# A hybrid trunk's attention: fp32r tiles and fp32r transposes for the softmax weights of the first half

## The chip, the cores and the metric

The kernel runs on one core of one Trainium2 chip. The metric is device time in microseconds (us), the median of repeated runs. The profile and its trace show one execution, with the engines PE (matmuls; PEld its weight loads), DVE (VectorE), ACT (ScalarE), POOL (GpSimd) and SP (SyncE).

## What is computed

A trunk of two layers over 1024 latent tokens and 256 context tokens, of width 1024: a convolution layer and an attention layer, each followed by a dense SwiGLU layer, all in fp32. The change lies in the attention, of which the core is this:

```python
def gqa_sdpa(q, k, v):                      # 16 query heads, 4 kv heads, head width 64
    qg = q.reshape(B, Q, N_KV_HEADS, KV_GROUP, Dh)
    s = jnp.einsum("bqkgd,bskd->bkgqs", qg, k).astype(jnp.float32) * (Dh ** -0.5)
    p = jax.nn.softmax(s, axis=-1).astype(v.dtype)
    o = jnp.einsum("bkgqs,bskd->bqkgd", p, v)
    return o.reshape(B, Q, H * Dh)
```

Each query reads all 1280 keys (1024 latent and 256 context), and the output passes through a projection `wo`.

## The kernel before

**Products in pairs.** The kernel keeps the operands of its matmuls as a high part, the fp32 value cast to the type fp32r, and a low part, the difference to the fp32 value, and sums the products of the parts. ACT casts, DVE subtracts.

**Units.** The 1024 queries run in two halves of 512. A half has 16 units: a kv head t and a block of 128 queries, and in a unit the four query heads that share t. `attn_stream` makes the list of steps. In a unit `scores` (L1105) does, for each head, six matmul rows against 1280 keys (L1116) into PSUM, DVE's scaling into the head's softmax slot in SBUF with the row's minimum beside it (L1122), and ACT's exponent in place, with the row sum (L1124). `values` (L1128) then takes the four slots through ten key blocks: PE transposes the block of each head, 128x128, into one PSUM bank (L1134, four transposes in f32 against an identity), ACT copies the bank as the high part (L1137), DVE subtracts for the low part (L1138), and PE adds both to the output (L1140, L1141). Two banks take the transposes in turn, four buffer pairs the parts. At the end of the unit come the reciprocal of the sums (DVE, L1145), its spread on POOL (L1147), two copies and two adds (ACT L1151, DVE L1152), two transposes and the product (L1155, L1156), and the store to `od` (POOL, L1450). The `values` of a unit run beside the `scores` of the next: three, three, three and two steps of it behind each of its heads (`turns`). The value products carry a later priority (`later`, 40 steps). A scheduler fixes from this one order for each engine, and waits are put where data or buffers ask for them; every engine then works through its own list in order.

**The slots.** The first half's slots come from a ring of places in three big tiles, T1, HS and T5 (`pring`). Units 0 to 2 run beside the last query projection; from unit 3 on attention runs alone. A unit takes four slots that the unit before does not hold, one by one. A slot is taken over when the first transpose of the last key block to read it is done, since the scaling of the next user writes it.

**Around it.** The queries of a unit come by a DMA on POOL's queue (L1102). When the first half is done, `out_proj` loads its output from `od` into the tile HS (L1485), splits it into high and low parts in tiles tagged T6 and T3 (`split`: ACT L161, DVE L164), and multiplies by `wo` (L172 to L174), beside the second half's attention, which uses slots of T1 and T5 again.

## Time and profile before

| | |
|---|---|
| median of 3 runs | 2941.39 us (2937.71 to 2943.6) |
| profiled execution | 2938.98 us |
| its span, first to last instruction | 2937.2 us |
| mean granted TensorE clock | 0.987 |
| busy: PE, PEld, DVE, ACT, POOL | 97%, 83%, 74%, 45%, 8% |
| first half, units 4 to 14 (1671.35 to 1833.42) | 162.07 us |
| f32 transposes L1134 in the trace | 1280 |

A row of a group gives line, engine, operation, tiles and shapes, count, then busy time and mean ns of one, then the idle time before them with what ended it. A timeline row gives start, duration, engine, line, operation, and in square brackets the idle time ahead of it and its releaser; x2 is two in a row. The ends of matmuls are modelled, so for PE and DVE the distance from start to start says more than a duration.

### The profile page before, as it was taken

To read this page: it belongs to the slowest core of one execution; us is meant where nothing else is said; L and a number is where in the kernel's file an instruction comes from. 1 tells how busy PE (TensorE), PEld (TensorE's weight loads), DVE (VectorE), ACT (ScalarE), POOL (GpSimd) and SP (SyncE) were. 2 spreads that over 40 slices of the span, in tenths; PEclk is the share of its full clock that TensorE was granted. 3 is DMA by queue.
4 is the path that set the end of the run, shared out by engine and by line. 5 is a ranking of instruction groups with operands and counts; after the bars stand their busy time and mean duration, and the time that the engine had idled before them with its cause. 6 is when DMAs were issued, how large, how long until landed. Compare 5 with 4: busy or idle time off the path is not lost.

```text
span 2937.2 us, 42731 instructions
## 1 busy us (share of the span) xinstructions
PE 2847.7 (97%) x16462; PEld 2446.1 (83%) x16462; DVE 2160.7 (74%) x3746; ACT 1335.5 (45%) x2229; POOL 222.6 (8%) x377
## 2 busy tenths in 40 slices
PE   7999989999999999999999999989999999999998
PEld 6888877888888889989888787767777778889997
DVE  6887788847556378877786899786666666786777
ACT  5222255532222245544445688645555543444444
POOL 0000001011022001000011111110000000010000
PEclk9999999999999999999999999999999999999999
DMA  6443444334356224333345211322222143353332
GB/s 249 140 120 98 116 131 145 135 116 143 115 175 198 65 74 165 114 104 112 109 156 170 88 46 46 97 87 81 66 73 83 60 149 99 110 170 104 102 98 75
DMA packets 131755, 336.58 MB, mean 115 GB/s; under 512 B 31328, under 2 KB 52864, under 8 KB 130656
## 3 DMA queue, kind: packets, MB, share of 16 engines
q1 hardware_dynamic: 78016, 222.33, 24.1%
q0 software_dynamic: 29344, 103.83, 10.7%
q10 hardware_dynamic: 24192, 7.70, 1.1%
q8 instruction: 129, 2.11, 0.3%
q14 instruction: 74, 0.61, 0.1%
HBM read 289.50 MB, written 38.93 MB: 112 GB/s over the span
## 4 chain that ended last, share of the span: by engine, by line
PE 86%; DVE 7%; ACT 2%; issue 2%; DMA 2%; ACTq 0%; POOL 0%; SPq 0%; DVEq 0%; POOLq 0%
PE ps L172 15%; PE ps L173 15%; PE ps L174 15%; PE ps L875 4%; PE ps L877 4%; PE ps L876 4%; PE ps L1116 4%; PE ps L1134 4%; PE ps L1140 2%; PE ps L454 2%; PE ps L455 2%; PE ps L456 2%; PE ps L1141 2%; PE ps L185 1%; PE ps L183 1%
## 5 line engine op out<-in xcount | busy, mean ns | idle before, releaser
L172 PE MATMUL ps<-T,wh 128*128 128x512 f32 (+1 forms) x1360 | 502.5, 370 | 1.4 <-ACT T L161 0.8
L174 PE MATMUL ps<-T,wl 128*128 128x512 f32 (+1 forms) x1360 | 500.4, 368 | 2.0 <-DVE wl L148 2.0
L173 PE MATMUL ps<-T,wh 128*128 128x512 f32 (+1 forms) x1312 | 481.4, 367 | 0.2 <-DVE T L164 0.2
L144 ACT CAST wh<-wr 128x1024 fp32r<-128x1024 f32 (+1 forms) x217 | 225.0, 1037 | 419.9 <-PE ps L173 307.2
L148 DVE TENSOR_TENSOR wl<-wr,wh 128x1024 fp32r<-128x1024 f32 (+1 forms) x217 | 261.9, 1207 | 168.5 <-ACT wh L144 167.1
L875 PE MATMUL ps<-T,wh 128*128 128x256 f32 x1092 | 310.7, 285 | 5.0 <-ACT wh L161 4.5
L876 PE MATMUL ps<-T,wh 128*128 128x256 f32 x1092 | 306.5, 281 | 0.0
L877 PE MATMUL ps<-T,wl 128*128 128x256 f32 x1092 | 305.4, 281 | 0.2 <-DVE wl L164 0.2
L1138 DVE TENSOR_TENSOR T<-ps,T 128x512 fp32r<-128x512 f32 x320 | 216.8, 687 | 107.6 <-ACT T L1137 106.8
L172 PEld LDWEIGHTS ps<-T,wh 128*128 128x128 f32 x1360 | 257.8, 190 | 43.7 <-ACT T L1506 1.7
L174 PEld LDWEIGHTS ps<-T,wl 128*128 128x128 f32 x1360 | 257.7, 190 | 42.4 <-DVE wl L148 2.2
L173 PEld LDWEIGHTS ps<-T,wh 128*128 128x128 f32 x1312 | 248.5, 189 | 38.2 <-DVE T L164 1.3
L1137 ACT CAST T<-ps 128x512 fp32r<-128x512 f32 x320 | 186.0, 586 | 191.1 <-PE ps L1134 177.6
L173 PE MATMUL ps<-HS,wh 128*128 128x512 f32 x656 | 257.9, 393 | 0.0
L172 PE MATMUL ps<-HS,wh 128*128 128x512 f32 x608 | 238.4, 392 | 0.9 <-ACT wh L144 0.9
L174 PE MATMUL ps<-HS,wl 128*128 128x512 f32 x608 | 237.5, 391 | 0.0
L875 PEld LDWEIGHTS ps<-T,wh 128*128 128x128 f32 x1092 | 206.1, 189 | 11.2 <-ACT wh L161 6.7
L876 PEld LDWEIGHTS ps<-T,wh 128*128 128x128 f32 x1092 | 206.6, 189 | 0.5
L877 PEld LDWEIGHTS ps<-T,wl 128*128 128x128 f32 x1092 | 206.2, 189 | 0.6 <-DVE wl L164 0.4
L1134 PE MATMUL ps<-cst,T 128*128 128x128 f32 x1100 | 189.6, 275 | 3.2 <-DVE T L1138 3.1
L1122 DVE TENSOR_SCALAR_CACHE_REDUCE T<-ps,rq 128x1280 f32<-128x1280 f32 x110 | 170.0, 1546 | 27.9 <-PE ps L1116 22.1
L1134 PEld LDWEIGHTS ps<-cst,T 128*128 128x128 f32 x1100 | 132.6, 141 | 49.5 <-DVE T L1138 30.8
(377 smaller groups left out, 6195.9 us busy)
## 6 DMA issues: line engine op xcount, KB each, us to landing
wr<-in_w SPq DMA_DIRECT2D x170, 512.0 KB, 3.6
wr<-in_pw SPq DMA_DIRECT2D x35, 512.0 KB, 3.5
HV<-in_wmodT POOLq DMA_DIRECT2D x56, 256.0 KB, 4.1
q<-in_wmodT POOLq DMA_DIRECT2D x56, 256.0 KB, 3.9
KB<-in_w SPq DMA_DIRECT2D x24, 512.0 KB, 3.6
HR<-in_w SPq DMA_DIRECT2D x23, 512.0 KB, 3.7
q<-in_w SPq DMA_DIRECT2D x23, 512.0 KB, 4.2
q<-qsd POOLq DMA_DIRECT2D x32, 256.0 KB, 3.3
```

What stands on the lines that cost most here:

```text
L144: nc.scalar.copy(hi, raw)
L148: nc.vector.tensor_tensor(lo, raw, hi.bitcast(F32), op=ALU.subtract)
L172: nc.tensor.matmul(out[:, :n], lhsT=wh, rhs=xh, start=k == 0, stop=False)
L173: nc.tensor.matmul(out[:, :n], lhsT=wh, rhs=xl, start=False, stop=False)
L174: nc.tensor.matmul(out[:, :n], lhsT=wl, rhs=xh, start=False, stop=k == nk - 1)
L875: nc.tensor.matmul(out, lhsT=wh, rhs=bh, start=first and k == 0, stop=False, **skip)
L876: nc.tensor.matmul(out, lhsT=wh, rhs=bl, start=False, stop=False, **skip)
L877: nc.tensor.matmul(out, lhsT=wl, rhs=bh, start=False, stop=k == 3, **skip)
L1122: nc.vector.tensor_scalar(out=pt, in0=sc, scalar1=rq[:, h:h + 1], scalar2=None, op0=ALU.mult, op1=ALU.min, accum_out=mn)
L1134: nc.tensor.transpose(tp[:, h * P:(h + 1) * P], Ps[h][:, j * P:(j + 1) * P], c["ident"])
L1137: nc.scalar.copy(ph, tp)
L1138: nc.vector.tensor_tensor(pl, tp, ph.bitcast(F32), op=ALU.subtract)
```

## The change

Units 4 to 15 of the first half no longer take slots of a shared ring. Each unit opens tiles of its own in one of two groups in turn: three heads in T1 and one in T4, or three in T5 and one in T6. `places` is called twice for a unit: first for F32 tiles, into which the scaling and the exponent go, and then for tiles over the same bytes of type fp32r, which the transposes read. Each fp32r tile is opened by a write of two columns behind the data (an ACT copy from the identity; 24 of them). The transposes of these units (480 of 1280) then run with fp32r operands, against an fp32r identity `idr` that is made once. Unit 3 takes T5 and T6 in f32. A tile is taken over as a whole: the first head of a unit waits for the last reader of all three heads of the tile. The second half's slots are two new tiles in T1 and T5, and its transposes stay in f32. HS is no longer used for slots after unit 2. `part`, a small tile of another stage, has one buffer and not two.

Lines of the kernel after stand two to four further on in `values`: L1134 becomes L1136 (fp32r) or L1138 (f32), L1137 becomes L1141, L1138 becomes L1142, L1140 and L1141 become L1144 and L1145, L1145 becomes L1149, L1152 becomes L1156, L1156 becomes L1160. L1116, L1122, L1124 and L161 to L174 keep theirs.

```diff
@@ values
-                nc.tensor.transpose(tp[:, h * P:(h + 1) * P], Ps[h][:, j * P:(j + 1) * P], c["ident"])
+                pt, to = Ps[h][:, j * P:(j + 1) * P], tp[:, h * P:(h + 1) * P]
+                if pt.dtype == F32R:
+                    nc.tensor.transpose(to.bitcast(F32R), pt, self.idr)
+                else:
+                    nc.tensor.transpose(to, pt, c["ident"])
@@ new
+    def places(self, dt):
+        out = []
+        for tag, m in self.groups[self.gi % 2]:
+            t = self.T(tag, [P, m * TOK + 2], dt)
+            if dt == F32R:
+                self.nc.scalar.copy(t[:, m * TOK:], self.idr[:, 0:2].bitcast(F32))
+            out += [t[:, i * TOK:(i + 1) * TOK] for i in range(m)]
+        return out
@@ attn_stream
+            own = self.groups is not None and waited
+            waited = self.groups is not None
+            if own:
+                slots, free = self.places(F32), self.pring
...
+            if own:
+                Ps = self.places(F32R)
+                self.gi += 1
             prev = self.values(t, Ps, sums, *dst_of(t, qt))
@@ attention
+        self.idr = self.cp.tile([P, P], F32R, tag="idr", name="idr")
+        nc.scalar.copy(self.idr, c["ident"])
+        self.groups = None
...
                 pr4 = self.T("T5", [P, 3, TOK])
-                self.pring = self.pring[:4] + [pr4[:, 0], pr4[:, 1], pr4[:, 2]] + self.pring[4:]
+                p6 = self.T("T6", [P, 1, TOK])
+                self.pring = [pr4[:, 0], pr4[:, 1], pr4[:, 2], p6[:, 0]]
+                self.gi = 0
+                self.groups = [(("T1", 3), ("T4", 1)), (("T5", 3), ("T6", 1))]
...
+        self.groups = None
+        pr1, pr4 = self.T("T1", [P, 3, TOK]), self.T("T5", [P, 3, TOK])
```

On DVE, from the third scaling of a unit to the first of the next, in the third group of four units. Tiles have their tag and a number; `ps` is PSUM, T2 the parts, `sb` and `sums` the unit's end. Before:

```order
L1122 TENSOR_SCALAR HS_13570,mn_15168<-ps_72,rq2_10629 128x1280
L1152 TENSOR_TENSOR sb_14960<-ps_72,sb_15084 64x256
L1138 TENSOR_TENSOR T2_13571<-ps_72,T2_13571 128x512
L1156 TENSOR_TENSOR sb_14960<-sb_14960,ps_72 128x256
L1122 TENSOR_SCALAR T1_13569,mn_15201<-ps_72,rq2_10629 128x1280
L1138 TENSOR_TENSOR T2_13571<-ps_72,T2_13571 128x512 x2
L1145 RECIPROCAL sums_14964<-sums_14964 128x4
L1145 RECIPROCAL sums_15095<-sums_15095 128x4
L1138 TENSOR_TENSOR T2_13571<-ps_72,T2_13571 128x512 x4
L1122 TENSOR_SCALAR T1_13569,mn_15233<-ps_72,rq2_10629 128x1280
```

And now, in the same place of a unit (this one of the fourth group):

```order
L1122 TENSOR_SCALAR T1_15682,mn_15757<-ps_72,rq3_10630 128x1280
L1156 TENSOR_TENSOR sb_15543<-ps_72,sb_15667 64x256
L1142 TENSOR_TENSOR T2_13571<-ps_72,T2_13571 128x512
L1160 TENSOR_TENSOR sb_15543<-sb_15543,ps_72 128x256
L1142 TENSOR_TENSOR T2_13571<-ps_72,T2_13571 128x512
L1122 TENSOR_SCALAR T4_15683,mn_15790<-ps_72,rq3_10630 128x1280
L1142 TENSOR_TENSOR T2_13571<-ps_72,T2_13571 128x512 x2
L1149 RECIPROCAL sums_15684<-sums_15684 128x4
L1142 TENSOR_TENSOR T2_13571<-ps_72,T2_13571 128x512 x2
L1122 TENSOR_SCALAR T5_15818,mn_15827<-ps_72,rq3_10630 128x1280
```

Before, units came in two kinds in turn, of which this one has six subtractions and two reciprocals behind its fourth scaling and the next one fewer. Now all units have this one order, four subtractions and one reciprocal, and the last scaling shown, the first head's in a new tile T5, waits for transposes of the unit two before it.

The other place is the end of the first half, again on DVE: the splits (L164, into T6 as the high part's tile and T3) and the last unit's end (`olast`). Before:

```order
L164 TENSOR_TENSOR T3_15975<-HS_15969,T6_15974 128x512 x3
L1138 TENSOR_TENSOR T2_13571<-ps_72,T2_13571 128x512 x2
L164 TENSOR_TENSOR T3_15975<-HS_15969,T6_15974 128x512 x2
L1138 TENSOR_TENSOR T2_13571<-ps_72,T2_13571 128x512 x2
L164 TENSOR_TENSOR T3_15975<-HS_15969,T6_15974 128x512
L1122 TENSOR_SCALAR T1_13569,mn_16003<-ps_72,rq0_10627 128x1280
L1138 TENSOR_TENSOR T2_13571<-ps_72,T2_13571 128x512 x2
L164 TENSOR_TENSOR T3_15975<-HS_15969,T6_15974 128x2x384
L1152 TENSOR_TENSOR olast_13573<-ps_72,sb_15961 64x256
```

And now:

```order
L1142 TENSOR_TENSOR T2_13571<-ps_72,T2_13571 128x512 x5
L1122 TENSOR_SCALAR T5_16045,mn_16089<-ps_72,rq0_10627 128x1280
L1142 TENSOR_TENSOR T2_13571<-ps_72,T2_13571 128x512
L164 TENSOR_TENSOR T3_16052<-HS_16046,T6_16051 128x512 x2
L1156 TENSOR_TENSOR olast_13575<-ps_72,sb_16036 64x256
L164 TENSOR_TENSOR T3_16052<-HS_16046,T6_16051 128x512 x2
L1156 TENSOR_TENSOR olast_13575<-ps_72,sb_16036 64x256
L164 TENSOR_TENSOR T3_16052<-HS_16046,T6_16051 128x512
L1160 TENSOR_TENSOR olast_13575<-olast_13575,ps_72 128x256
L164 TENSOR_TENSOR T3_16052<-HS_16046,T6_16051 128x512
L164 TENSOR_TENSOR T3_16052<-HS_16046,T6_16051 128x2x384
```

The splits stood among the last unit's subtractions; now they stand behind all of them. On POOL's queue the first three of the four loads of HS (L1485, now L1513) have moved up between the q loads of units 7 to 14.

More of the change, by code (lines that the diff above doesn't have):

```diff
@@ L109, in acc, with tiny @@
         return self.sp.tile([P, 512], F32, tag="acc", name="acc", bufs=2)[:, :n]
-    def tiny(self, shape, name):
-        return self.sp.tile(shape, F32, tag=name, name=name, bufs=2)
+    def tiny(self, shape, name, bufs=2):
+        return self.sp.tile(shape, F32, tag=name, name=name, bufs=bufs)
     @contextmanager
@@ L582, in shift @@
         nc, cv = self.nc, self.cvs["C"]
-        self.part = self.tiny([P, NC_], "part")
+        self.part = self.tiny([P, NC_], "part", 1)
         nc.vector.tensor_scalar(out=self.part, in0=self.vsum[:, :NC_], scalar1=KT / (KT - 1.0), scalar2=None,
@@ L1158, in values @@
         yield 0.1
+    def places(self, dt):
[6 more added lines that the diff above has]
+        return out
     def attn_stream(self, units, kts, dst_of, loaded=False):
-        prev, cur, nq, Ps = None, None, None, []
+        prev, cur, nq, Ps, waited = None, None, None, [], False
         for n, (t, qt) in enumerate(units):
```

## The prediction

> **What bounds the kernel now.** The profiled execution took 2938.98 us, 2937.2 of it the span, 1.78 around it; the three timed runs have their median at 2941.39, 2.41 above. The sums below are differences against the profiled execution; I add them to the median. About 0.2%, 5.9 us, is what a measurement here can tell from no change. The change touches units 3 to 15 of the first half's attention, so I read that stretch first, by a window of two units (us, then busy time and count on PE, PEld, DVE, ACT, POOL, then clock, DMA share, GB/s).
>
> ```profile
> 1706.50:1735.91 29.41, 28.63 (x174) 23.50 (x173) 26.86 (x45) 23.91 (x42) 4.83 (x8) 1.00 0.29 72
> ```
>
> A unit takes 14.7 us, with PE busy 97% of it, DVE 91%, ACT 81%, at full clock. PE looks like the bound, but the ends of matmuls are modelled, so I ask who waits. Two groups of eight units (1706.5 to 1824.15) answer: busy time and mean ns, then the idle time before them and what ended it.
>
> ```profile
> L1138 DVE TENSOR_TENSOR T<-ps,T 128x512 fp32r<-128x512 f32 x80 | 53.3, 685 | 8.3 <-ACT T L1137 8.1
> L1137 ACT CAST T<-ps 128x512 fp32r<-128x512 f32 x80 | 46.1, 586 | 19.8 <-PE ps L1134 12.3 <-PE ps L1140 4.9
> ```
>
> The engines pass one block round a ring: PE transposes (L1134), ACT copies the high part (L1137), DVE subtracts (L1138), PE transposes into the bank that came free. DVE waits about 1 us a unit for ACT and ACT 1.5 us for the transposes, while PE waits for hardly anything that shows. A faster transpose can pay only where one stands in this ring with DVE waiting behind it. The order on DVE says where; these rows are DVE's timeline.
>
> ```profile
> 1660.03 1.53 DVE L1122 TENSOR_SCALAR_CACHE_REDUCE T<-ps,rq 128x1280 f32<-128x1280 f32 x1
> 1661.60 0.43 DVE L1152 TENSOR_TENSOR sb<-ps,sb 64x256 f32<-64x256 f32 x1
> 1662.06 0.69 DVE L1138 TENSOR_TENSOR T<-ps,T 128x512 fp32r<-128x512 f32 x1
> 1662.99 0.68 DVE L1138 TENSOR_TENSOR T<-ps,T 128x512 fp32r<-128x512 f32 x1
> 1663.60 1.54 DVE L1122 TENSOR_SCALAR_CACHE_REDUCE T<-ps,rq 128x1280 f32<-128x1280 f32 x1
> ...
> 1670.08 1.36 DVE L1138 TENSOR_TENSOR T<-ps,T 128x512 fp32r<-128x512 f32 x2 [0.53 <-ACT T L1137]
> 1671.35 1.54 DVE L1122 TENSOR_SCALAR_CACHE_REDUCE HS<-ps,rq 128x1280 f32<-128x1280 f32 x1
> 1672.82 1.28 DVE L1138 TENSOR_TENSOR T<-ps,T 128x512 fp32r<-128x512 f32 x2
> 1674.02 1.54 DVE L1122 TENSOR_SCALAR_CACHE_REDUCE T<-ps,rq 128x1280 f32<-128x1280 f32 x1
> 1675.82 1.27 DVE L1138 TENSOR_TENSOR T<-ps,T 128x512 fp32r<-128x512 f32 x2
> 1677.02 1.53 DVE L1122 TENSOR_SCALAR_CACHE_REDUCE HS<-ps,rq 128x1280 f32<-128x1280 f32 x1
> ...
> 1679.99 1.54 DVE L1122 TENSOR_SCALAR_CACHE_REDUCE T<-ps,rq 128x1280 f32<-128x1280 f32 x1
> 1683.22 0.18 DVE L1145 RECIPROCAL sums<-sums 128x4 f32<-128x4 f32 x1 [0.48 <-ACT T L1124]
> 1683.70 1.37 DVE L1138 TENSOR_TENSOR T<-ps,T 128x512 fp32r<-128x512 f32 x2 [0.31 <-ACT T L1137]
> ...
> 1833.42 1.54 DVE L1122 TENSOR_SCALAR_CACHE_REDUCE T<-ps,rq 128x1280 f32<-128x1280 f32 x1
> ```
>
> From unit 4's first scaling (1671.35) to unit 15's (1833.42) are 162.07 us, eleven units: 14.73 each. The rest of the sum goes by such starts.
>
> **The new unit, step by step.** After the change each unit has one fixed order on DVE, between its four scalings (h0 to h3): two subtractions; one subtraction, an L1152, a subtraction; L1152, subtraction, L1156, subtraction; and after h3 two subtractions, the reciprocal, two subtractions. Before, the two kinds of unit alternated. I price each stretch by the rows above that have the same work. From h0 to h1: 1674.02 - 1671.35 = 2.67. From h1 to h2: 1677.02 - 1674.02 = 3.00. From h2 to h3: 1663.60 - 1660.03 = 3.57, in which some 0.15 are small gaps, so 3.4 at the least.
>
> From h3 to the next h0 lies the dear stretch, and it holds a wait that the change lengthens. The softmax tile is now taken over whole: the next unit's first scaling writes a tile of three heads, and is let go by the third transpose of the last key block of the unit two before it; before, each slot came free by itself, with the first transpose to read it. That transpose in turn needs the bank freed by the last subtraction ahead of the scaling. So: h3 at 1679.99, the two subtractions behind the reciprocal at 1683.70, the second of them at 1683.70 + 1.37 - 0.69 = 1684.38. From a subtraction's start to the transposes that it lets go, and from a group's last transpose to its reader, by these rows of PE and ACT (with DVE's 1670.08):
>
> ```profile
> 1670.86 0.29 PE L1134 MATMUL ps<-cst,HS 128*128 128x128 f32 x1
> ...
> 1671.21 0.27 PE L1134 MATMUL ps<-cst,T 128*128 128x128 f32 x1
> ```
>
> ```profile
> 1671.52 0.59 ACT L1137 CAST T<-ps 128x512 fp32r<-128x512 f32 x1 [0.80 <-PE ps L1134]
> ```
>
> 0.78 from subtraction to transpose, 0.31 from the fourth transpose (1671.21) to the copy. Now the transposes' own pace. In f32 they follow each other by 0.11; for fp32r the nearest rows are the convolution's short products.
>
> ```profile
> 1751.72 0.28 PE L1134 MATMUL ps<-cst,HS 128*128 128x128 f32 x1
> 1751.83 0.27 PE L1134 MATMUL ps<-cst,T 128*128 128x128 f32 x1
> ```
>
> ```profile
> 110.65 0.24 PE L533 MATMUL ps<-HS,T 128*128 128x162 f32 x1
> 110.72 0.35 PE L532 MATMUL ps<-HS,T 128*128 128x324 f32 x1
> ```
>
> ```profile
> 1713.84 0.42 PEld L1134 LDWEIGHTS ps<-cst,T 128*128 128x128 f32 x4 [0.23 <-DVE T L1138]
> 110.65 0.19 PEld L532 LDWEIGHTS ps<-HS,T 128*128 128x128 f32 x1
> 110.76 0.19 PEld L533 LDWEIGHTS ps<-HS,T 128*128 128x128 f32 x1
> ```
>
> 162 fp32r columns take 0.07, so 128 take 0.055: half of 0.11. Against that stand the weight loads: those of the fp32r products begin 0.11 apart and last 0.19, which would keep a transpose at 0.11; those of the f32 transposes last 0.14 and come as close as (0.42 - 0.14) / 3 = 0.09. The trace of before shows no fp32r transpose, so its pace lies between 0.055 and 0.11; I take 0.06, because the load of a transpose is already the quicker kind, and keep both ends. The Trainium skill bears on it from both sides: "TensorE: Matmul & The Clock Gate", section "LDWEIGHTS (loading the stationary operand)", gives columns / 1.2 in ns, 107 for 128 columns, which would mean no gain; its section "Back-to-back issue gap" gives about 81 ns for a sustained stream at 128 columns, by which two transposes more would cost 0.04 more a unit than by my 0.06. The row of loads at 0.09 disagrees with the first.
>
> So the next h0 starts at 1684.38 + 0.78 + 2 x 0.06 + 0.31 = 1685.59, 5.60 after h3. A unit is 2.67 + 3.00 + 3.57 + 5.60 = 14.84, with the gaps of the third stretch closed 14.67; I take the middle, 14.77. Eleven times 0.04 is +0.5 us. What the change saves on PE, 40 x 0.05 = 2.0 us a unit, appears nowhere in this sum: PE merely waits more. That is the heart of the forecast. At 0.11 a transpose the same sum gives 14.87 and +1.5 us.
>
> **Edits at nothing, and the ends of the stretch.** The 24 casts of two columns go to ACT, which is 19% idle; I bound each by 0 and by the nearest short row, DVE's L1145 at 0.18, and at their place, behind h3's exponent, ACT has 0.8 of slack (row 1671.52), which covers them; without that cover they would cost 2 x 0.18 a unit. Three of the four loads of the attention output (HS<-od, POOL) now start while units still run, between the q loads. The group of q loads in the same eight units:
>
> ```profile
> L1102 POOL DMA_DIRECT2D q<-qsd x8 | 6.2, 770 | 53.6 <-PE ps L1116 48.6 <-PE ps L1134 5.1
> ```
>
> POOL waits 53.6 of the eight units' 117.65 us for PE to let the next q go; so I bound the three loads by 0 and, if each held a q load up by as much as one issue takes, by 3 x 0.77, and take 0, since those waits hide them. At the end, the split of the attention output takes tag T6, which unit 15 now holds: the splits, before put between that unit's subtractions, all come after them.
>
> ```profile
> 1854.06 1.89 DVE L164 TENSOR_TENSOR T<-HS,T 128x512 fp32r<-128x512 f32 x3
> ```
>
> ```profile
> 1862.09 0.50 PE L1140 MATMUL ps<-T,HR 128*128 128x512 f32 x1 [1.18 <-ACT T L1137]
> 1864.30 0.39 PE L172 MATMUL ps<-T,wh 128*128 128x512 f32 x1
> ```
>
> The work is the same (six splits of 128x512, by the row of three 0.63 each, 3.8 us of DVE). Unit 15's subtractions come earlier by as much as the splits come later, and the output projection needs only the first split to begin, so I leave L172 at about 1864.3 from unit 15's start: 0, with 1.5 either way. Second half and everything else keep their order: 0.
>
> **The rivals.** Faster: the ring shortens everywhere, not only at h0. For it: ACT's 12.3 us of waits for transposes in eight units, 1.5 a unit, each wait being for four transposes of which half pace saves 0.2 of 0.44; of 1.5 that is 0.7, and if DVE gets most of it, 0.6 a unit, 11 units give -6.6: 2934.8. Against: in the rows of h3 to h0, ACT's two copies run straight behind the exponent, and no transpose is late there. Slower: PE stands still at h0. In the new order the score products of h1 and one value product (L1141 of before) queue on PE behind the late scaling, and the next unit's transposes behind them. PE's work of a unit is 28.63 / 2 = 14.3 by busy time; if transposes stay at 0.11 and that stall is over 1 us, a unit takes 15.3, eleven times 0.57 is +6.3, 2947.7. It decides from a stall of about 1 us on; with the 2 us saved there is room for it. Third, the change doesn't do what it says: weight loads 0.11 apart hold the transposes at their old pace and nothing stalls, +1.5, 2942.9. This is what the Trainium skill's section "LDWEIGHTS (loading the stationary operand)" of "TensorE: Matmul & The Clock Gate" would make of it.
>
> **How the numbers follow.** Forecast 0.52 (+0.5, 2941.9; its own bounds 2938 to 2945 by -0.06 and +0.11 a unit and the 1.5 of the end), faster rival 0.22, slower rival 0.17, no faster transposes 0.09. The range reaches into both outer rivals: 2933.5 to 2948.5. Faster by over 0.2% is the first rival, 0.23 with a tail of the forecast; slower is the second with the like, 0.19; the rest, 0.58, is no change.
>
> **What would show it.** Right: a settled unit of 14.7 to 14.85 us; h3 to h0 near 5.6, with DVE idle about 0.6 before h0 and PE named as its releaser; fp32r transposes 0.06 apart; PE's busy share down by a tenth and its idle time up. Wrong: h3 to h0 at 5.1 or below, transposes 0.11 apart, or L172 first run later than 32.5 us after unit 15's first scaling (before: 1864.30 - 1833.42 = 30.88).

## The result, and the profile after

The changed kernel takes 2945.86 us (median of 20 runs, 2941.3 to 2948.38), the kernel before, on the same chip, 2940.91 (20 runs, 2937.17 to 2943.6). The ratio is 1.0018, 95% interval 1.0012 to 1.0025: +4.95 us. That is inside the 0.2% called no change and inside the range, but ten times the +0.5 that was forecast, and by the interval it is a small loss. The profiled execution took 2945.39 us.

The page of after, its engines:

```profile
PE 2847.1 (97%) x16462; PEld 2440.4 (83%) x16462; DVE 2161.4 (73%) x3746; ACT 1340.9 (46%) x2254; POOL 223.0 (8%) x377
```

Two units of after, by a window as before's:

```profile
1706.50:1736.66 30.16, 27.62 (x174) 21.90 (x174) 26.95 (x45) 24.81 (x45) 4.82 (x8) 1.00 0.28 71
```

Two units now take 30.16 us where they took 29.41, at the same clock. PE's busy time fell by 1.0 (28.63 to 27.62) and its share from 97% to 92%; DVE's busy time is the same. So in two units PE stands idle for 2.54 us where it was 0.78, and DVE for 3.21 where it was 2.55. Which waits those are, the groups and the waits of after say, in the same stretch of 117.65 us (now 7.8 units):

```profile
L1142 DVE TENSOR_TENSOR T<-ps,T 128x512 fp32r<-128x512 f32 x79 | 52.0, 683 | 3.9 <-ACT T L1141 3.6
L1141 ACT CAST T<-ps 128x512 fp32r<-128x512 f32 x78 | 45.0, 588 | 11.5 <-PE ps L1136 8.2 <-PE ps L1144 2.1
```

```profile
DVE T L1122 <- PE ps L1136: 5.9, 8, 0.7
PE ps L1116 <- DVE T L1122: 10.1, 16, 0.9
```

The subtraction's wait for ACT fell from 8.1 to 3.6, the cast's wait for transposes from 12.3 to 8.2. That looks like the faster transposes at work, but f32_new_order below has nearly the same two figures with f32 transposes: it goes with the new order. New is the wait of the first line of the second block, and that of its second line has grown (in before PE's score products waited 3.1 for scalings in this stretch). Once a unit the scaling waits 0.7 us for a transpose, and then PE's score products wait for the scaling.

One unit on DVE (its timeline, from first scaling to first scaling; rows of the unit's end left out):

```profile
1746.45 1.55 DVE L1122 TENSOR_SCALAR_CACHE_REDUCE T<-ps,rq 128x1280 f32<-128x1280 f32 x1 [0.74 <-PE ps L1136]
...
1749.12 1.54 DVE L1122 TENSOR_SCALAR_CACHE_REDUCE T<-ps,rq 128x1280 f32<-128x1280 f32 x1
...
1752.21 1.53 DVE L1122 TENSOR_SCALAR_CACHE_REDUCE T<-ps,rq 128x1280 f32<-128x1280 f32 x1
...
1755.78 1.54 DVE L1122 TENSOR_SCALAR_CACHE_REDUCE T<-ps,rq 128x1280 f32<-128x1280 f32 x1
1757.24 1.28 DVE L1142 TENSOR_TENSOR T<-ps,T 128x512 fp32r<-128x512 f32 x2
1758.85 0.18 DVE L1149 RECIPROCAL sums<-sums 128x4 f32<-128x4 f32 x1 [0.33 <-ACT T L1124]
1759.48 1.30 DVE L1142 TENSOR_TENSOR T<-ps,T 128x512 fp32r<-128x512 f32 x2 [0.45 <-ACT T L1141]
1761.52 1.55 DVE L1122 TENSOR_SCALAR_CACHE_REDUCE T<-ps,rq 128x1280 f32<-128x1280 f32 x1 [0.74 <-PE ps L1136]
```

The stretches are 2.67, 3.09, 3.57 and 5.74; over the nine settled units (6 to 14) the mean unit is 15.08. Units 4 and 5 still take 15.69 and 13.22, so the eleven units take 164.62, 2.55 more than before.

Why the last stretch is longer than forecast stands on PE's timeline of the same place:

```profile
1760.03 0.63 PE L1116 MATMUL ps<-KB,q 128*128 128x512 f32 x2
1760.50 0.46 PE L1136 MATMUL ps<-idr,T 128*128 128x128 f32 x4
1760.80 0.47 PE L1145 MATMUL ps<-T,HR 128*128 128x512 f32 x1
1761.11 0.46 PE L1136 MATMUL ps<-idr,T 128*128 128x128 f32 x4
```

The first subtraction behind the reciprocal starts at 1759.48; its transposes should follow 0.78 later, at 1760.26. They start at 1760.50, because two score products (1760.03) stand ahead of them on PE, which runs without a gap here. The second pair slips with the first: subtraction at 1759.48 + 1.30 - 0.69 = 1760.09, transposes at 1761.11, 1.02 later.

The pace of the transposes can't be read off the duration of a merged row, since the last of the four has a duration of its own. Narrow windows inside the group at 1760.50 give rows that begin with its second, third and fourth transpose:

```profile
1760.57 0.40 PE L1136 MATMUL ps<-idr,T 128*128 128x128 f32 x3
1760.63 0.33 PE L1136 MATMUL ps<-idr,T 128*128 128x128 f32 x2
1760.71 0.25 PE L1136 MATMUL ps<-idr,T 128*128 128x128 f32 x1
```

The third starts 0.13 behind the first (1760.50) and the fourth 0.21, where f32 transposes at 0.11 take 0.22 and 0.33. In a run of eight (in lav20 below, the first at 1696.63) the pace settles; its fourth and its eighth:

```profile
1696.83 0.41 PE L1136 MATMUL ps<-idr,T 128*128 128x128 f32 x3
1697.17 0.24 PE L1136 MATMUL ps<-idr,T 128*128 128x128 f32 x1
```

That is 0.34 in four steps, 0.085 each. The loads, third and fourth of a group, first in before (the group at 1713.84 of the prediction), then in after:

```profile
1714.01 0.14 PEld L1134 LDWEIGHTS ps<-cst,T 128*128 128x128 f32 x1
1714.12 0.14 PEld L1134 LDWEIGHTS ps<-cst,T 128*128 128x128 f32 x1
```

```profile
1758.46 0.14 PEld L1136 LDWEIGHTS ps<-idr,T 128*128 128x128 f32 x1
1758.55 0.14 PEld L1136 LDWEIGHTS ps<-idr,T 128*128 128x128 f32 x1
```

So f32 loads follow each other by 0.11 and fp32r loads by 0.09 (0.085 in lav20's run of eight).

The rest of the loss lies at the end of the half. Unit 15's first scaling and the output projection's first product, in after and in a second execution of the same kernel (after_again, below):

```profile
1836.90 1.55 DVE L1122 TENSOR_SCALAR_CACHE_REDUCE T<-ps,rq 128x1280 f32<-128x1280 f32 x1 [0.75 <-PE ps L1136]
1869.97 0.39 PE L172 MATMUL ps<-T,wh 128*128 128x512 f32 x1
```

```profile
1835.46 1.55 DVE L1122 TENSOR_SCALAR_CACHE_REDUCE T<-ps,rq 128x1280 f32<-128x1280 f32 x1 [0.74 <-PE ps L1136]
1867.13 0.39 PE L172 MATMUL ps<-T,wh 128*128 128x512 f32 x1
```

From scaling to projection are 30.88 us before, 33.07 and 31.68 after. The difference of 1.39 between the two executions of one kernel is the clock: in a window of 8 us the granted clock is 0.79 in the first and 1.00 in the second, and up to 1859.3, within that window, the starts on DVE agree to 0.03 us, counted from unit 15's first scaling.

```profile
1856.00:1864.00 8.00, 6.90 (x38) 5.17 (x36) 4.82 (x9) 3.73 (x8) 1.46 (x2) 0.79 0.05 16
```

```profile
1856.00:1864.00 8.00, 7.11 (x46) 5.30 (x44) 5.31 (x9) 4.24 (x9) 1.46 (x2) 1.00 0.22 59
```

So +0.80 is the change's, the rest comes and goes. Then the projection itself, its first group of products from first to last (one line of it; before, then after):

```profile
L172 PE MATMUL ps<-T,wh x64: 388/397/505, 1864.3 to 1926.8; 128*128 128x512 f32 x64
```

```profile
L172 PE MATMUL ps<-T,wh x64: 388/397/502, 1870.0 to 1933.6; 128*128 128x512 f32 x64
```

62.5 us became 63.6. PE's timeline of after names two waits there which before's did not have, 0.25 and 0.79, 1.04 together: one for a split, one for an exponent of the second half's attention, which runs beside the projection.

```profile
1875.23 0.50 PE L173 MATMUL ps<-T,wh 128*128 128x512 f32 x1 [0.25 <-DVE T L164]
...
1878.93 0.33 PE L1138 MATMUL ps<-cst,T 128*128 128x128 f32 x1 [0.79 <-ACT T L1124]
```

The account of the +4.95: unit 3, just ahead, 14.41 for 14.26, +0.15; units +2.55; end of the half +0.80; projection +1.1; together +4.6. What lies ahead of unit 3 and behind these products differs from before by up to 0.8 either way, in each of the two executions of after.

### The profile page after: what moved, and what is told of

It is laid out like the page before. It is cut to its first block, busy times and chain, and to the rows that moved or that the text cites. A ratio compares the mean times of both kernels' runs of the same rounds, so it can differ in the third digit from the quotient of the medians.

```text
span 2943.6 us, 42746 instructions
## 1 busy us (share of the span) xinstructions
PE 2847.1 (97%) x16462; PEld 2440.4 (83%) x16462; DVE 2161.4 (73%) x3746; ACT 1340.9 (46%) x2254; POOL 223.0 (8%) x377
## 4 chain that ended last, share of the span: by engine, by line
PE 87%; DVE 8%; ACT 2%; issue 2%; DMA 1%; ACTq 0%; SPq 0%; DVEq 0%
PE ps L172 15%; PE ps L173 15%; PE ps L174 15%; PE ps L875 4%; PE ps L877 4%; PE ps L876 4%; PE ps L1116 4%; PE ps L1138 3%; PE ps L1144 2%; PE ps L1145 2%; PE ps L454 2%; PE ps L456 2%; PE ps L455 2%; PE ps L185 1%; PE ps L183 1%
## 5 line engine op out<-in xcount | busy, mean ns | idle before, releaser
L174 PE MATMUL ps<-T,wl 128*128 128x512 f32 (+1 forms) x1360 | 501.5, 369 | 2.0 <-DVE wl L148 2.0
L172 PE MATMUL ps<-T,wh 128*128 128x512 f32 (+1 forms) x1360 | 502.8, 370 | 0.5 <-DVE sm L839 0.4
L1142 DVE TENSOR_TENSOR T<-ps,T 128x512 fp32r<-128x512 f32 x320 | 216.1, 686 | 106.0 <-ACT T L1141 105.1
L172 PEld LDWEIGHTS ps<-T,wh 128*128 128x128 f32 x1360 | 258.3, 190 | 42.2 <-ACT T L1534 1.2
L174 PEld LDWEIGHTS ps<-T,wl 128*128 128x128 f32 x1360 | 258.2, 190 | 41.8 <-DVE wl L148 2.2
L1141 ACT CAST T<-ps 128x512 fp32r<-128x512 f32 x320 | 186.3, 587 | 185.8 <-PE ps L1138 160.8
L172 PE MATMUL ps<-HS,wh 128*128 128x512 f32 x608 | 238.4, 392 | 0.9 <-ACT wh L144 0.9
L174 PE MATMUL ps<-HS,wl 128*128 128x512 f32 x608 | 237.4, 391 | 0.0
L1122 DVE TENSOR_SCALAR_CACHE_REDUCE T<-ps,rq 128x1280 f32<-128x1280 f32 x122 | 188.4, 1545 | 35.6 <-PE ps L1116 22.4
L1124 ACT ACTIVATE T<-T,mn 128x1280 f32<-128x1280 f32 x122 | 166.8, 1367 | 53.8 <-DVE T L1122 51.8
L926 DVE TENSOR_TENSOR T<-ps,T 128x512 f32<-128x512 f32 (+1 forms) x168 | 110.0, 661 | 67.8 <-PE ps L174 66.0
```

The lines of the kernel that those rows point to most:

```text
L172: nc.tensor.matmul(out[:, :n], lhsT=wh, rhs=xh, start=k == 0, stop=False)
L174: nc.tensor.matmul(out[:, :n], lhsT=wl, rhs=xh, start=False, stop=k == nk - 1)
L1122: nc.vector.tensor_scalar(out=pt, in0=sc, scalar1=rq[:, h:h + 1], scalar2=None, op0=ALU.mult, op1=ALU.min, accum_out=mn)
L1124: nc.scalar.activation(pt, pt, AF.Exp, bias=mn, scale=-1.0, accum_out=sums[:, 0, h:h + 1])
L1141: nc.scalar.copy(ph, tp)
L1142: nc.vector.tensor_tensor(pl, tp, ph.bitcast(F32), op=ALU.subtract)
```

## The experiments

Two things arrive with this change that the diff does not part: the tiles are taken over whole, and the transposes are fp32r. With them comes a third, which no line of the diff writes: another order of instructions. Theories were: the taking over of whole tiles costs the time (by the wait at h0); the new order costs it; the faster transposes give something back; a wait removed at one place of the ring returns at another. Where a kernel has the tie named below, two tiny transposes of the opening columns, ahead of a unit's first two key blocks, keep those blocks behind the opening write; they shift the kernel's line numbers by one to three.

**a_f32: the new tiles, f32 transposes.**

```diff
             if own:
-                Ps = self.places(F32R)
                 self.gi += 1
```

> The new tiles and groups stay, but no second, fp32r tile is opened: the transposes read the F32 tiles and run in f32 (no casts of two columns either). On DVE the order becomes the alternating one of the kernel before. Theory 1 (the wait for the taken-over tile at h0 costs, whatever the order): the first scaling of a unit still waits for the third transpose of the last key block two units before, two f32 transposes at 0.11 later than in fp32r, so a unit takes 15.1 us or more and the time is 2946 to 2950 us. Theory 2 (the new order on DVE costs, the tiles don't): a unit takes 14.7 as before, and what is left is the end of the half, 2941 to 2944 us.

Measured: 2942.44 us beside 2939.77, 1.0007 (0.9998 to 1.0016). DVE's order is the alternating one of before again, and so are the units: 15.70 and 13.74 in turn, 14.72 on average. Its window of two units:

```profile
1706.50:1735.94 29.44, 28.63 (x176) 23.44 (x173) 26.85 (x45) 23.97 (x41) 4.82 (x8) 1.00 0.29 72
```

The whole-tile groups alone cost a unit next to nothing (14.72 for before's 14.70). And the scheduler writes this program in another order than after, though it differs only in the type of the transposes and in the second tiles and small casts that go with it; which of these moves the order was not parted.

**b_8: eight places that come free one by one, f32.** Instead of groups, the ring of places simply gets eight.

```diff
-                p6 = self.T("T6", [P, 1, TOK])
-                self.pring = [pr4[:, 0], pr4[:, 1], pr4[:, 2], p6[:, 0]]
-                self.gi = 0
-                self.groups = [(("T1", 3), ("T4", 1)), (("T5", 3), ("T6", 1))]
+                p1, p4, p6 = self.T("T1", [P, 3, TOK]), self.T("T4", [P, 1, TOK]), self.T("T6", [P, 1, TOK])
+                self.pring = [pr4[:, 0], pr4[:, 1], pr4[:, 2], p6[:, 0], p1[:, 0], p1[:, 1], p1[:, 2], p4[:, 0]]
```

> The same eight places as F32 slots of lasting tiles, each taken over by itself as before the change, transposes in f32; order on DVE as in the run with f32 transposes in new tiles. Beside that run it shows the price of taking over a tile as a whole. Theory 1: the first scaling waits for the first transpose and not for the third, 2 x 0.11 a unit, some 2.5 us less than the run with new tiles. Theory 2: no difference, 14.7 a unit, both about 2941 to 2944 us.

Measured: 2942.52, 1.0009 (1.0000 to 1.0018); units 15.80 and 13.61, 14.70. Neither the width of what is taken over nor the number of places bounds the old order. Both f32 kernels still lose some 2.7 us by their medians, at the edge of what the intervals tell, with units that equal before's: from unit 15's first scaling to the projection they take 31.42 and 31.43 (+0.55), for the projection's products 63.9 each (+1.4). So a loss at the end comes without fp32r too. It does not come with the new tiles alone either: f32_new_order, which has a_f32's tiles and type in another order, takes 30.75 to the projection, and a_first 29.14.

**a_3grp_g: three groups in turn, with the tie.** A tile is then taken over from the unit three before, so the wait at h0 should go.

```diff
-        for tag, m in self.groups[self.gi % 2]:
+        for tag, m in self.groups[self.gi % 3]:
...
-                self.groups = [(("T1", 3), ("T4", 1)), (("T5", 3), ("T6", 1))]
+                self.groups = [(("T1", 3), ("T6", 1)), (("HS", 4),), (("T5", 3), ("T4", 1))]
```

> Three groups in place of two: T1+T6, HS as a tile of four heads, T5+T4, in turn, so that a unit takes over the tiles of the unit three before it; transposes in fp32r; two tiny transposes a unit of the two opening columns tie the first blocks to the opening write. Theory 1: the wait of 0.74 us at h0 is gone, a unit takes about 14.35 us, 9 us less over the half than the change, 2937 us. Theory 2: the tiles don't matter; the order on DVE is again an alternating one, so about 14.7 a unit, 2941 us.

Measured: 2948.0, 1.0024 (1.0013 to 1.0034); the gain that was looked for did not come. The scalings run ahead (units of 11.63 to 13.61 behind the first), the subtractions are owed, and the wait is back later with the same length, at unit 13 and at the second half's first scaling. The first of them on DVE (L1138 is the fp32r transpose here):

```profile
1795.62 1.55 DVE L1122 TENSOR_SCALAR_CACHE_REDUCE T<-ps,rq 128x1280 f32<-128x1280 f32 x1 [0.74 <-PE ps L1138]
```

The eleven units take 152.48, the end 47.33: 199.8 together, where after has 164.62 + 33.07 = 197.7. In both the clock was lowered at the end, here about twice as long (0.72 and 0.86 in two neighbouring windows of 8 us); with after's 1.4 taken off, and an estimated 2.8 here, 197.0 stand against 196.3. A place more lets the scalings run further ahead; the owed work comes due at the end. Unit 14 also holds HS, into which the projection's loads go, and what that costs was not measured.

**a_first: the single tile first in each group.** The next unit's first scaling then waits for one head's tile and not for three heads'.

```diff
-                self.groups = [(("T1", 3), ("T4", 1)), (("T5", 3), ("T6", 1))]
+                self.groups = [(("T4", 1), ("T1", 3)), (("T6", 1), ("T5", 3))]
```

> The change with the single tile for the first head and the tile of three for the others. The first scaling of a unit now waits for one transpose of the last key block, not for three; the order on DVE stays that of the change. Theory 1: two transposes less at 0.057, 0.11 a unit, 1.3 us less than the change, 2944.5 us. A third theory (the width of the taken-over tile is what costs, 0.35 a unit): back to 14.7 a unit, 2942 us.

Measured: 2942.14, 1.0007 (0.9998 to 1.0016): 2.4 above the kernel before beside it, where after is 4.95 above. The settled unit is 14.92, with 5.57 for the last stretch and 0.59 before h0:

```profile
1759.62 1.55 DVE L1122 TENSOR_SCALAR_CACHE_REDUCE T<-ps,rq 128x1280 f32<-128x1280 f32 x1 [0.59 <-PE ps L1136]
```

The wait at h0 is 0.15 shorter and the unit 0.16, a little more than the 0.11 expected: the scaling is let go by the first of four transposes and not the third, which start 0.13 apart. The rest was not expected and sits at the rim: units 3 to 14 take 178.16 (before 176.32, after 179.03), and from unit 15 to the projection 29.14, 1.74 less than before; the projection's products then take 64.8, 2.3 more than before.

**lav20: the value products' later priority halved, from 40 steps to 20.** This changes the order while the transposes stay fp32r.

```diff
                 self.groups = [(("T1", 3), ("T4", 1)), (("T5", 3), ("T6", 1))]
+                self.lav = 20
```

> The change with the value products' later priority at 20 steps in place of 40 in the first half alone. On DVE every unit then has three subtractions between the reciprocal and the next unit's first scaling, not two, so that a subtraction stands in the place where DVE now waits 0.74 us for the taken-over tile. Theory 1 (that wait is what the units pay): most of it is covered, a unit takes about 14.5 us, 7 us less than the change, 2939 us. Theory 4 (the ring of transpose, copy and subtraction has its own length, and a wait taken away at one place comes back at the next): a unit stays at 15.0 to 15.1, 2945 us.

Measured: 2948.64 beside 2939.86, 1.0028 (1.0018 to 1.0038); units 15.17. No scaling waits for a transpose now, but between two scalings DVE stands still four times, for ACT:

```profile
1748.37 0.18 DVE L1149 RECIPROCAL sums<-sums 128x4 f32<-128x4 f32 x1 [0.41 <-ACT T L1124]
1749.20 0.69 DVE L1142 TENSOR_TENSOR T<-ps,T 128x512 fp32r<-128x512 f32 x1 [0.66 <-ACT T L1141]
1750.06 0.69 DVE L1142 TENSOR_TENSOR T<-ps,T 128x512 fp32r<-128x512 f32 x1 [0.16 <-ACT T L1141]
1751.14 0.69 DVE L1142 TENSOR_TENSOR T<-ps,T 128x512 fp32r<-128x512 f32 x1 [0.39 <-ACT T L1141]
```

1.62 in place of after's 0.33 + 0.45 + 0.74 = 1.52. The wait at h0 is one place where the ring's slack shows, not a cost that goes when the wait goes.

**lav20_f32: the same with f32 transposes.** Both edits, that of a_f32 and that of lav20.

> The same later priority of 20 with transposes in f32 from the F32 tiles (no second tile, no small casts). The order on DVE is the same for all units as in the run with fp32r, but for one subtraction that moves behind the reciprocal, so the pair shows what the pace of the transposes is worth under one order. By the pace in the ring: each block's four transposes end 0.2 us later, and where they stand in the chain (two to four times a unit) a unit gets 0.3 to 0.8 us longer, 15.3 to 15.8, 2949 to 2954 us. If the transposes are off the ring, both runs take the same time within 1 us.

Measured: 2960.6, 1.0070 (1.0056 to 1.0084); units 16.27, longer than expected. DVE's order differs from lav20's in the place of one subtraction, but PE's order differs by more. Here PE does the first transpose of a group at 1764.00 and the other three only at 1765.50, behind six score products and a value product, and DVE stands still behind that group:

```profile
1766.99 1.29 DVE L1142 TENSOR_TENSOR T<-ps,T 128x512 fp32r<-128x512 f32 x2 [1.19 <-ACT T L1141]
```

So the difference of 16.27 - 15.17 = 1.10 us a unit is the type's with all that the scheduler makes of it on PE. It does not give the worth of the pace.

**swap_tail: T4 and T6 exchanged, with the tie.** Unit 15 then does not hold T6, which the splits need.

```diff
-                self.groups = [(("T1", 3), ("T4", 1)), (("T5", 3), ("T6", 1))]
+                self.groups = [(("T1", 3), ("T6", 1)), (("T5", 3), ("T4", 1))]
```

> The change with the single tiles exchanged (T1+T6 and T5+T4), so that the last unit does not hold T6 and the splits of the attention output need not wait for its transposes; two tiny transposes a unit of the opening columns as in the run with three groups. If the held tile T6 is what the end of the half costs, the output projection starts 2 us earlier after unit 15's first scaling (33.1 in the change, 30.9 before) and the time is 2943 to 2944 us. If it is not, 2946 us as the change.

Measured: 2948.4, 1.0028 (1.0018 to 1.0038); units 15.04 but 16.83 and 14.70 in the first two, and 34.13 from unit 15 to the projection. The lowered clock shows in this trace too (0.88 and 0.91 in two neighbouring windows of 8 us, together as much as after's 0.79 in one); less the 1.4 that it cost there, the stretch is an estimated 32.7, still longer than after_again's 31.68. That T6 is held by unit 15 is not what this stretch costs; a miss. The projection's products, though, take 62.2, and neither of after's two waits is among them:

```profile
L172 PE MATMUL ps<-T,wh x64: 388/397/505, 1872.1 to 1934.3; 128*128 128x512 f32 x64
```

From unit 15 to the last of these products are 96.3, an estimated 94.9 at full clock; after_again has 95.3 and before 93.4. With T6 free the two waits go, but much of what they cost seems to come back ahead of the projection.

**after_again: the changed kernel once more, one execution.** No edit.

> The changed kernel itself once more, for a second trace: units of 15.07 us again; if the halved clock at 1856 to 1864 us in its first trace belongs to the kernel, it is there again at that place; if it fell there by chance, the output projection starts 31.5 us after unit 15's first scaling and not 33.1.

Measured: 2943.32 us, units 15.07, 31.68 from unit 15 to the projection (its rows stand above). The units repeat to 0.01, the end does not, by the clock.

**f32_new_order: after's DVE order, f32 transposes.** The instructions on DVE are recorded and chained in the order in which after has them; the scheduler may not move them. PE's and ACT's order it still chooses.

```diff
-                Ps = self.places(F32R)
...
+    def pin(self, order):
+        at, last = dict(S=16, D=29, R=4, F=4, G=2), None
+        for x in order:
+            ins = self.dv[x][at[x]].ins
+            at[x] += 1
+            if last is not None:
+                self.tc.add_manual_dep(ins, last.name, mybir.DependencyInfo(
+                    mybir.DependencyClass.NoSync, mybir.DependencyReason.DATA), reason="order")
+            last = ins
```

Called behind the loop, with one letter for each instruction: S a scaling, D a subtraction, R a reciprocal, F and G the unit's end. A settled unit reads SDDSDFDSFDGSDDRDD.

> New tiles, f32 transposes, and DVE's order pinned to that of the change. If the pace of the transposes matters under the new order as it did with the priority of 20 (1.1 a unit), a unit takes 15.6 to 16.2 and the time is 2952 to 2958 us: then the new order costs about 1 us a unit and fp32r gives most of it back. If PE's pace is off the path, 15.1 to 15.2, 2946 to 2948 us.

Measured: 2952.29 beside 2940.68, 1.0038 (1.0025 to 1.0052). Units 15.78: 2.68, 3.06, 3.57 as in after, and 6.47 for the last stretch. On DVE and PE at that place:

```profile
1762.99 1.37 DVE L1142 TENSOR_TENSOR T<-ps,T 128x512 fp32r<-128x512 f32 x2 [0.52 <-ACT T L1141]
...
1765.70 1.55 DVE L1122 TENSOR_SCALAR_CACHE_REDUCE T<-ps,rq 128x1280 f32<-128x1280 f32 x1 [1.34 <-PE ps L1116]
```

```profile
1764.46 0.61 PE L1138 MATMUL ps<-cst,T 128*128 128x128 f32 x4
1764.83 0.48 PE L1144 MATMUL ps<-T,HR 128*128 128x512 f32 x1
1765.14 0.40 PE L1145 MATMUL ps<-T,HR 128*128 128x512 f32 x1
1765.38 0.28 PE L1116 MATMUL ps<-KB,q 128*128 128x256 f32 x1
```

Here h0 waits 1.34, and the releaser is no transpose but h0's own last score product (1765.38). The scheduler put it on PE behind the last transposes and two value products, where after has its score products ahead of those transposes; PE runs without a gap in that stretch, though over two units it is busy only 29.23 of 31.56 us.

The subtraction's wait for ACT and the cast's wait for transposes are after's, with f32 transposes: 3.6 and 8.4 where after has 3.6 and 8.2. What differs on DVE is the wait at h0, 9.4 for 5.9.

```profile
L1142 DVE TENSOR_TENSOR T<-ps,T 128x512 fp32r<-128x512 f32 x75 | 50.0, 684 | 3.9 <-ACT T L1141 3.6
L1141 ACT CAST T<-ps 128x512 fp32r<-128x512 f32 x75 | 43.1, 587 | 15.7 <-PE ps L1138 8.4 <-PE ps L1144 4.6
L1122 DVE TENSOR_SCALAR_CACHE_REDUCE T<-ps,rq 128x1280 f32<-128x1280 f32 x31 | 47.8, 1541 | 9.4 <-PE ps L1116 9.4
```

So with f32 DVE's new order, with the order on PE that the scheduler wrote beside it, costs 15.78 - 14.72 = 1.06 a unit, and after is 15.78 - 15.08 = 0.70 shorter. By these rows that 0.70 is not the pace. The last four transposes stand no later here than in after: the third starts at 1764.46 + 2 x 0.11 = 1764.68, and with after's 0.28 from its third transpose to the scaling (1761.11 + 0.13 = 1761.24, and 1761.52) h0 would have started at an estimated 1764.96, 5.73 behind h3 (1765.70 - 6.47 = 1759.23), as in after. What comes on top is the place of one score product on PE. Had it stood ahead of the transposes, it would have put them off by about the 0.12 that it takes (1765.38 to the next start at 1765.50), so under after's order on PE the pace is worth an estimated 0.1 a unit; no run has that order with f32.

**fp32r_old_order: before's DVE order, fp32r, with the tie.** The same edit with the string of the old order and `places(F32R)` kept.

> The change's tiles and fp32r transposes with DVE's order pinned, from unit 4's first scaling to unit 15's last, to the alternating order of the kernel before (two tiny transposes a unit tie the first blocks to the opening write). With the run of f32 transposes in new tiles (old order, 14.73 a unit), the change (new order, fp32r, 15.07) and the run sent beside this one (new order, f32), each order stands with each pace. If the order is what costs: a unit falls below 14.73 by what the pace is worth there, 0.2 to 0.8, 14.0 to 14.5, and the time is 2934 to 2940 us, faster than both kernels. If the order costs nothing and DVE is bound by the chain of scaling, exponent, copy and subtraction: 14.7 to 15.0 a unit, 2942 to 2946 us.

Measured: 2946.52 beside 2940.68, 1.0018 (1.0009 to 1.0027); units 13.70 and 16.23, 14.97. The old order did not come out at 14.72 or below. The rows of the scalings give 2.92 and 3.28 where a_f32 has 2.68 and 3.00, and the casts wait 15.7 us for transposes in the stretch of 117.65, where before has 12.3 and after 8.2: with DVE held to the old order, the faster transposes did not reach ACT earlier. PE's and ACT's orders were still the scheduler's, and the tie was in it, so this says little of the pace alone.

**fp32r_all_old: all three orders as in a_f32, with the tie.** Scores, transposes, products, exponents and casts are chained too.

```diff
+        self.pin(" S16 D29 D30 S17 F4 D31 D32 S18 F5 D33 G2 S19 D34 D35 R4 D36 D37 D38 D39 S20 D40 F6 D41 S21"
...
+        self.pin(" E16 A31 C4 A32 E17 C5 A33 E18 A34 A35 E19 A36 A37 A38 A39 A40 A41 C6 E20 C7 A42 A43 E21 A44"
...
+        self.pin(" Q96 T100 T101 T102 T103 L23 T104 T105 T106 T107 H24 L24 H25 Q97 Q98 Q99 Q100 Q101 T108 T109 T110 T111 L25 T112"
...
```

> As the run with fp32r and DVE's old order, but PE's and ACT's orders are pinned too, all three to those of the run with f32 transposes in new tiles; so beside that run (14.72 a unit) only the pace of the transposes differs (and two tiny transposes a unit), and beside the run with DVE pinned alone (14.97) only PE's and ACT's order. If PE's order was what held the transposes back behind score products there, and the pace is worth what the rows say: the long stretch of 7.05 us holds three to four groups of transposes in a row, 0.2 us less each, and a unit falls to 14.2 to 14.5, the time to 2937 to 2940 us. If the pace is worth nothing in the old order, 14.7 and 2942 us; if something in fp32r itself makes it longer, 14.9 and 2945 us.

Measured: 2944.09 beside 2940.64, 1.0012 (1.0002 to 1.0021); units 13.42 and 16.44, 14.93. One stretch of each pair is 3.62 where a_f32 has 2.68, and the waits name what it holds: the tie (its line is L1135 here) waits for the small cast of two columns, which comes late on ACT.

```profile
PEld ps L1135 <- ACT T L1172: 3.7, 4, 0.9
```

The 0.94 belongs to the tie, which after does not have. If it were the whole price of the tie, the rest of a pair would be 29.86 - 0.94 = 28.92, 14.46 a unit, with gains in two other stretches (6.84 for a_f32's 7.05, 4.15 for 4.38).

**fp32r_all_old_2: the small casts chained right behind their exponents.**

```diff
+        self.pin(" E16 A31 C4 A32 E17 C5 A33 E18 K0 A34 A35 E19 K1 A36 A37 A38 A39 A40 A41 C6 E20 C7 A42 A43"
...
```

> As the run with fp32r and all three orders old, with the small casts pinned on ACT too, each right behind the exponent of its tile. In that run one stretch of every second unit (first scaling to second) was 3.62 us where the f32 run has 2.68: on PE a tiny transpose waited 0.9 us for a small cast that ACT did only after the copies. If that wait of the experiment's own tie was the whole loss, the stretch is 2.7 again, the gains of the others (6.84 for 7.05, 4.15 for 4.38) stay, a unit takes 14.4 to 14.5 and the time is 2939 to 2941 us, about the kernel before and 2 to 3 below the run with f32. If the loss is elsewhere, a unit stays at 14.7 to 14.9, 2944 us.

Measured: 2944.41 beside 2939.74, 1.0012 (1.0003 to 1.0022); units 13.65 and 16.34, 15.00. The tie still waits, 0.6 each time, and the same stretch is 3.28:

```profile
PEld ps L1135 <- ACT T L1172: 2.4, 4, 0.6
```

The gains did not stay: those stretches are 7.08 and 4.39 here. The same sum gives 29.99 - 0.60 = 29.39 a pair, 14.70 a unit, so in the run before, what the tie held up seems to have come back as the gains. What fp32r would give in the old order without the tie is not measured; the two sums say 14.46 and 14.70, against a_f32's 14.72, and a gain is not shown.

## Why the prediction came out as it did

The time fell into the range, and no change was the likeliest class. The forecast's own bounds did not hold: 2945.86 lies above its 2945 (its figures give 2939.2 to 2944.1, and the middle of 14.84 and 14.67 is 14.76), and only the reach into the slower rival's side holds the time. The steps, one by one:

**One order for all units, and h0 waiting for a transpose: right.** All settled units are alike, DVE stands 0.74 before h0 (forecast about 0.6), and PE's transpose is named as releaser. The first two, units 4 and 5, have other orders, which the sum of eleven equal units left out.

**"A unit is 2.67 + 3.00 + 3.57 + 5.60 = 14.84, with the gaps of the third stretch closed 14.67; I take the middle, 14.77": mis-sized.** It is 2.68 + 3.10 + 3.57 + 5.73 = 15.08. The small gaps did not close (+0.07 on the middle), the second stretch grew by 0.10, the last by 0.13. In the last, two score products stood ahead of the transposes on PE: 0.78 from subtraction to transpose became 1.02. Against that the subtraction came 0.08 earlier behind h3 (1760.09 - 1755.78 = 4.31 for 4.39), and from the first of the last transposes to the scaling are 0.41 for 0.43. The 0.78 came from a row of before where PE was free in time; the new order put more there. DVE's new order was in the sum, PE's was not. Why the second stretch grew stays open.

**The pace of 0.06: right where it stood.** The sum uses it for two steps, from the first to the third transpose, and these take 0.13 (1760.50 to 1760.63). The fourth follows by 0.08, and a longer run goes at 0.085, so as a pace for all transposes it is too low. The loads were misread in the prediction: the four of f32 transposes, 0.42 in all, are not 0.09 apart but 0.06, 0.11 and 0.11. The Trainium skill, "TensorE: Matmul & The Clock Gate", section "Back-to-back issue gap", gives about 81 ns for a sustained stream at 128 columns, and the 0.085 of lav20's run of eight agrees. The 107 ns of the Trainium skill's section "LDWEIGHTS (loading the stationary operand)" on the same page, by which nothing would have been gained, do not hold for the fp32r loads, which are 0.085 apart.

**"What the change saves on PE, 40 x 0.05 = 2.0 us a unit, appears nowhere in this sum: PE merely waits more": as the sum had it in after, and its worth is not parted.** PE's busy share fell from 97% to 92%, half of the tenth that was forecast, and the unit got no shorter. The two pairs that change the type under a like order on DVE (0.70 for f32_new_order and after, 1.10 under lav20's) change PE's order with it, and in the first the place of one score product makes up the difference by the rows. So neither speaks against the 0.10 that the sum gave for the pace, and neither proves it. With f32 the scheduler's order cost 1.06; the third rival's 14.87 for a unit that keeps the old pace was off by 0.9, since like the forecast it had no order on PE. The slower rival's 15.3 was nearer to f32_new_order's 15.78, but there DVE waits at h0 for a score product that PE does late, which is not the stall of PE that it described.

**Eleven units: +0.5 forecast, +2.55 measured.** The nine settled ones take 135.71 for before's 132.77, +2.9; the two ahead of them give 0.4 back, which is luck, since the sum did not have it.

**The end of the half "0, with 1.5 either way": +0.8, inside, and the projection +1.1, not thought of.** Both stand with f32 transposes as well in a_f32 and b_8 (+0.55 and +1.4), so they don't need fp32r; the end changes with the order too (30.75 in f32_new_order). The mark of 32.5 us for L172 was passed in the profiled execution (33.07) only with the lowered clock; at full clock it is 31.68. The projection's two waits are gone where T6 is free (swap_tail), at the price of a longer stretch ahead of it; what the end costs stays open.

**The faster rival** failed where it was strongest: the casts' waits for transposes did shrink (12.3 to 8.2), but by the order and not by the pace (8.4 in f32_new_order), and DVE's waiting moved to h0.

What is shown: whole-tile groups cost a unit next to nothing in the old order (a_f32, b_8); DVE's new order with f32, together with PE's that comes with it, costs 1.06 (f32_new_order); of the kernels in two groups with the priority step at 40 that were left to the scheduler, those with fp32r settle into the new order (after, a_first, swap_tail) and a_f32 does not. What is not shown: what the pace of the transposes is worth in either order. No version tried beats the kernel before; the nearest are a_first (2942.14) and a_f32 (2942.44), whose intervals include 1.

## What to carry to other kernels

Where a scheduler orders the instructions, a change of one operand's type is also a change of the order on every engine: price PE's new queue as well as DVE's, since a duration taken from a row of before holds only if the same work still stands ahead of it. To part the two, build the change with the old type, and chain the new order with the old type, on all engines: chained on DVE alone, the pair here still differed in PE's order, and its difference was the place of one product. And a wait at one place of a ring is where its slack shows: taken away there (a third group, a halved priority step) it came back elsewhere with the same length or more.

## What the runs showed of the hardware

Transposes of 128 columns whose operand is fp32r start 0.06 to 0.08 us apart in a group of four and settle at 0.085 in a run of eight (lav20), f32 ones start 0.11 apart; their weight loads follow each other by 0.085 and 0.11. So four fp32r transposes take 0.21 from the first to the last start and four f32 ones 0.33. And the granted clock was 0.79 in 8 us near the end of the half in one trace of after and 1.00 in another (after_again), which moved a stretch of 32 us by 1.4; swap_tail and a_3grp_g show the lowered clock there too. A single profiled execution can't carry a difference of that size at such a place.
